# Attention sums of the even layer taken for two tiles of queries at once, and the base weight block of the MLPs loaded two pieces ahead

## The chip, the cores and the metric

One core of a Trainium2 chip runs the whole program. The metric is the device time of one execution in microseconds (us), from the first instruction to the end; the profile's span is the part from the first to the last instruction of the engines.

## The reference

A two-layer encoder trunk on 256 tokens of width 1024. The even layer runs two groups of eight heads side by side, neighbourhood attention and multi-head latent attention (MLA), behind one input projection and one output projection. The odd layer is a mixture of dilated windows. Each layer is followed by a squared-ReLU MLP.

```python
def even_mixer(xn, ...):
    hcat = xn @ w_in
    out_a = neighbourhood_attention(q, k, v, rpb)          # 8 heads of 64
    out_b = dense_attention(q, k, v, 96 ** -0.5)           # 8 heads, 96 wide keys, 64 wide values
    return jnp.concatenate([out_a, out_b], axis=-1) @ w_o

def sq_relu_mlp(xn, w1, w2):
    return jnp.square(jax.nn.relu(xn @ w1)) @ w2
```

## The kernel before

Activations stay on the core with features on the 128 partitions and 256 tokens along the free axis, which are two tiles of 128 queries. Weights come from HBM in pieces of up to 1 MB. A product of full precision is made of three products of halves: `split` (L204) makes a high part on ScalarE and the remainder on VectorE, and `mm3` (L208) multiplies high by high, high by low and low by high. These matmuls use the whole 128 by 128 array.

**The even layer** (`even`, L564) runs two lists of steps that are woven into each other by cost estimates at its end. The main list holds the projections of the heads and then `out_steps` (L328), the output projection. The side list comes from `attention` (L834) and has 16 items in `items`: eight of the neighbourhood group (kind 0) and eight of MLA (kind 1), each for one tile `t` of 128 queries and one pair `hp` of heads. An item goes through three steps. `scores` (L783) multiplies queries by keys, adds the bias of kind 0, and normalises: VectorE reduces, ScalarE takes the exponential and scales, and the result is the tile `pp`. `turn_probs` (L812) transposes `pp` with four matmuls against the identity `ident`, and one copy brings the result to the tile `pts`. `mix` (L820) multiplies the values by `pts`: the two heads of the pair use one half of the array's columns each (64 of 128), and `split` then writes 128 columns to `mixed`, which `out_steps` reads. Scores of kind 0 (`two_heads`, L213) use the array as two halves of 64 rows; scores of kind 1 use all 128 columns and 96 rows through `mm3`.

```python
for n in range(len(items) + 2):
    for fn, m in ((scores, n), (turn_probs, n - 1), (mix, n - 2)):
```

**The MLPs** (`mlp`, L355) take their second weight in seven products for eight blocks, and so need sums of blocks. For pieces `j < 14` `load_weight` (L136) fetches the fourth block of 512 columns, the base, into a tile `sums` (three buffers, tag `sum`), GpSimd copies it beside itself, and a second transfer on GpSimd's queue adds two other blocks while it writes (`accum_op=ALU.add`). `weight` (L196) hands out a piece and asks `prefetch` to load `LOAD_AHEAD` = 4 pieces ahead and to split two ahead.

The order on each engine is not that of the program text: a scheduler places each instruction where its inputs and buffers are there by its own estimates, and an earlier place in the text counts only between instructions that could both go. `open_accs`, `bank("w")` and the like draw from rings of buffers.

Of the kernel before, what the change touches and what calls it, by code (L numbers as in the profile page):

```python
# [19 lines left out]
F32 = mybir.dt.float32  # L20
# [6 lines left out]
P = 128  # L27
D = 1024
KT = D // P
T = 256  # L30
NT = T // P
# [10 lines left out]
BLK = 512  # L42
LOAD_AHEAD = 4
# [6 lines left out]
def trunk(ctx, tc, a, out):  # L50
    nc = tc.nc
# [8 lines left out]
    def scratch(shape, name):  # L60

        n = int(np.prod(shape))
        v = work.tile([P, 512], F32, tag="scratch", name=name, bufs=12)[:, :n]
        if len(shape) == 2:
            v = v.rearrange("p (a b) -> p a b", b=shape[1])
        return v
# [8 lines left out]
    def quarter_pair(name):  # L75
        return [act.tile([P, KT // 2, T], F32R, tag="quarter", name=name + v, bufs=4) for v in "hl"]

    def bank(tag):
        return ps.tile([P, 512], F32, tag=tag, name=tag)
# [26 lines left out]
    specs = []  # L106
# [25 lines left out]

    parts = {}
    state = {"loaded": 0, "split": (0, 0), "used": 0, "pool": None, "parts_done": None}

    def load_weight(pieces=1, before=lambda i: None):  # L136
        j = state["loaded"]
        src, n, _, seven = specs[j]
        if seven:

            blocks = src.rearrange("p (b n) -> p b n", n=BLK)
            sums = state["pool"].tile([P, 2, BLK], F32, tag="sum", name="sum", bufs=3)
            nc.sync.dma_start(sums[:, 0, :], blocks[:, 3, :])
            nc.gpsimd.tensor_copy(out=sums[:, 1, :], in_=sums[:, 0, :])  # L144
            nc.gpsimd.dma_start(sums, blocks[:, 0:3:2, :], accum_op=ALU.add)
            n = 3 * BLK
        raw = wraw.tile([P, WCH], F32, tag="raw", name="raw")
        for i in range(pieces):
            c = slice(i * n // pieces, (i + 1) * n // pieces)
            before(i)  # L150
            nc.sync.dma_start(raw[:, c], src[:, c])
        parts[j] = [raw, None, None] + ([sums] if seven else [])
        state["loaded"] = j + 1
# [5 lines left out]
    def split_piece(eng=None):  # L159
        j, i = state["split"]  # L160
        _, _, n, seven = specs[j]
        state["split"] = (j, i + 1) if i < n - (not seven) else (j + 1, 0)
        if i == 0:
            parts[j][1:3] = (wsp.tile([P, WCH], F32R, tag=v, name=v) for v in ("whi", "wlo"))
            if seven:

                with tc.issue_after(state["parts_done"]):
                    more_sums(parts[j])
        if i == n:
            parts[j][1:3] = split_sums(parts[j])  # L170
            return
        raw, hi, lo = (z[:, cut(j, i, n)] for z in parts[j][:3])
        return split(hi, lo, raw, eng)
# [16 lines left out]
    def prefetch(loads, splits):  # L190
        while state["loaded"] < min(loads, len(specs)):
            load_weight()
        while state["split"] < (min(splits, len(specs)), 0):
            split_piece()

    def weight():  # L196

        j = state["used"]
        prefetch(j + 1, j + 1)
        prefetch(j + LOAD_AHEAD, j + SPLIT_AHEAD)  # L200
        state["used"] = j + 1
        return parts.pop(j)[1:3]

    def split(hi, lo, src, eng=None):  # L204
        a = nc.scalar.copy(hi, src).ins  # L205
        return a, (eng or nc.vector).tensor_tensor(lo, src, hi.bitcast(F32), op=ALU.subtract).ins  # L206
# [22 lines left out]
    def tok(t):  # L229
        return slice(t * P, (t + 1) * P)  # L230
# [333 lines left out]
    def even(ep):  # L564
# [208 lines left out]
        mixed = [quarter_pair("oa"), None]  # L773
        items = [(0, t, hp) for hp in range(4) for t in range(NT)] + [(1, t, hp) for hp in range(4) for t in range(NT)]
        biases, probs, turned = {}, {}, {}
# [7 lines left out]
        def scores(n):  # L783
            kind, t, hp = items[n]
            load_bias(n + 2)

            sb = [bank("w")[:, 0:T] for _ in range(2)] if kind == 0 else bank("w").rearrange("p (j n) -> p j n", j=2)
            s_of = lambda j: sb[j] if kind == 0 else sb[:, j]
            if kind == 0:
                two_heads(sb, *qk[hp], tok(t))  # L790
            else:
                for j in range(2):
                    h = 2 * hp + j
                    (qh, ql), (kh, kl) = mT["q"], mT["k"]
                    mm3(sb[:, j], qh[0:96, h, tok(t)], ql[0:96, h, tok(t)], kh[0:96, h, :], kl[0:96, h, :], True, True)
            pp, sn = scratch([2, T], "pp"), scratch([2, T], "sn")
            mn, z, rz = (work.tile([P, 2], F32, tag=v, name=v, bufs=3) for v in ("mn", "z", "rz"))
            for j in range(2):
                o = s_of(j)
                if kind == 0:  # L800
                    nc.vector.tensor_tensor_reduce(out=sn[:, j], in0=o, in1=biases[n][:, j, :], op0=ALU.add, op1=ALU.min,
                                                   scale=-1.0, scalar=3e38, accum_out=mn[:, j:j + 1])
                else:
                    nc.vector.tensor_scalar(sn[:, j], o, -MLA_SCALE, None, ALU.mult, ALU.min, accum_out=mn[:, j:j + 1])
            for j in range(2):
                nc.scalar.activation(pp[:, j], sn[:, j], AF.Exp, bias=mn[:, j:j + 1], scale=-1.0, accum_out=z[:, j:j + 1])
            nc.vector.reciprocal(rz, z)
            for j in range(2):
                nc.scalar.activation(pp[:, j], pp[:, j], AF.Copy, scale=rz[:, j:j + 1])
            probs[n] = pp  # L810
# [7 lines left out]
            nc.any.tensor_copy(out=turned[n], in_=pt.rearrange("p (b n) -> p b n", b=4))  # L818

        def mix(n):  # L820
            kind, t, hp = items[n]
            pts = turned.pop(n)
            if mixed[kind] is None:
                mixed[kind] = quarter_pair("ob")
            v = (vna, vml)[kind]
            pvo = bank("acc" if n < 6 else "w")
            for kk in range(NT):
                for j in range(2):
                    h = 2 * hp + j
                    nc.tensor.matmul(pvo[64 * j:64 * j + 64, 0:P], v[:, kk, h * 64:(h + 1) * 64], pts[:, 2 * j + kk, :],  # L830
                                     start=kk == 0, stop=kk == NT - 1)
            split(*(z[:, hp, tok(t)] for z in mixed[kind]), pvo[:, 0:P])

        def attention():  # L834

            out = []
            for n in range(len(items) + 2):
                for fn, m in ((scores, n), (turn_probs, n - 1), (mix, n - 2)):
                    if 0 <= m < len(items):
                        out.append(lambda fn=fn, m=m: fn(m))  # L840
                if n == 0:
                    out += [lambda: None] * 2
            return out
# [322 lines left out]
```

## Time and profile before

| | |
|---|---|
| median of 3 runs | 733.68 us (733.67 to 734.14) |
| the profiled execution: its time, its span | 733.63 us, 731.9 us |
| granted TensorE clock over the span | 0.998 |
| busy over the span: TensorE, weight loads | 723.1 us, 660.6 us |
| VectorE, ScalarE, GpSimd | 623.0 us, 522.6 us, 78.8 us |
| bytes read from HBM | 142.10 MB |

The even layer takes the first 112 us, its MLP and the hand-over the time to about 300 us, the odd layer goes to about 560 us and the second MLP to the end. The matmul rows give a start and a modelled length: the length of a lone row is longer than the distance to the next start, since matmuls overlap, so times are read from start to start. A row with "x8" is eight matmuls of one line in a row; a product of 32-bit operands with `pts` shows twice, so that the four matmuls of one `mix` are a row of eight.

### The profile page before, as it was taken

The page shows a single profiled execution, that of the slowest core. Times are in us where ns is not written, and L with a number is a line of the kernel's source. Part 1 is how long each engine was busy: PE and PEld are TensorE (multiplying, and loading weights), DVE is VectorE, ACT ScalarE, POOL GpSimd, SP SyncE. Part 2 cuts the span into 40 slices and gives each one's busy share as a digit, 9 for nine tenths or more (in the row PEclk, how much of TensorE's full clock was granted, in tenths as well). Part 3 has the DMA queues.
Part 4 walks back from the last instruction along what each step waited for, and adds up shares of the span by engine and source line. Part 5 has one row for each costly group of instructions (what it writes and reads, how often), then busy time and mean ns, then how long its engine had stood idle before and what let it go on. Part 6 is the DMA issues. An engine that isn't in the chain of part 4 may idle for free.

```text
span 731.9 us, 13834 instructions
## 1 busy us (share of the span) xinstructions
PE 723.1 (99%) x5234; PEld 660.6 (90%) x5234; DVE 623.0 (85%) x1188; ACT 522.6 (71%) x986; POOL 78.8 (11%) x73
## 2 busy tenths in 40 slices
PE   9999999999999999999999999999999999999996
PEld 6988899999999998989899899998999999999995
DVE  6888859999999959989777888778759998999956
ACT  7778968767767756878676767867658766766752
POOL 0100002224222000000000000000002422232000
PEclk9999999999999999999999999999999999999999
DMA  8773338798989644664655456455658798898611
GB/s 317 274 264 133 116 116 216 216 287 244 265 263 255 193 165 166 216 207 150 229 178 171 170 188 211 170 188 198 199 195 201 235 277 221 259 273 242 211 39 59
DMA packets 38499, 149.56 MB, mean 204 GB/s; under 512 B 5152, under 2 KB 7200, under 8 KB 29344
## 3 DMA queue, kind: packets, MB, share of 16 engines
q1 hardware_dynamic: 30384, 133.71, 52.0%
q0 software_dynamic: 7616, 14.68, 12.0%
q8 instruction: 41, 0.67, 0.4%
q10 hardware_dynamic: 432, 0.28, 0.1%
q14 instruction: 26, 0.21, 0.1%
HBM read 142.10 MB, written 1.05 MB: 196 GB/s over the span
## 4 chain that ended last, share of the span: by engine, by line
PE 83%; issue 10%; DVE 3%; DMA 2%; ACT 1%; POOL 0%; SPq 0%; POOLq 0%; DVEq 0%; ACTq 0%
PE acc L937 11%; PE acc L209 10%; PE w L209 10%; PE w L210 10%; PE w L211 10%; PE acc L210 10%; PE acc L211 9%; PE acc L938 5%; PE w L218 1%; PE w L1014 1%; DMA sum<-in_w 1%; PE acc L1029 1%; PE w L816 1%; PE w L830 1%; DMA raw<-in_w_cv 1%
## 5 line engine op out<-in xcount | busy, mean ns | idle before, releaser
L206 DVE TENSOR_TENSOR wlo<-raw,whi 128x512 fp32r<-128x512 f32 (+3 forms) x360 | 296.7, 845 | 51.3 <-ACT whi L205 51.1
L205 ACT CAST whi<-raw 128x512 fp32r<-128x512 f32 (+3 forms) x360 | 253.6, 746 | 86.7 <-PE w L210 59.0
L210 PE MATMUL w<-xx,whi 128*128 128x256 f32 x528 | 149.6, 283 | 0.0
L211 PE MATMUL w<-xx,wlo 128*128 128x256 f32 x528 | 149.3, 283 | 0.0
L209 PE MATMUL w<-xx,whi 128*128 128x256 f32 x528 | 148.9, 283 | 0.0
L937 PE MATMUL acc<-xx,whi 128*128 128x512 f32 x336 | 122.0, 404 | 0.0
L210 PEld LDWEIGHTS w<-xx,whi 128*128 128x128 f32 x528 | 101.2, 192 | 1.5 <-DVE xx L246 0.4
L209 PEld LDWEIGHTS w<-xx,whi 128*128 128x128 f32 x528 | 101.0, 192 | 1.1
L211 PEld LDWEIGHTS w<-xx,wlo 128*128 128x128 f32 x528 | 101.2, 192 | 0.0
L938 PE MATMUL acc<-xx,wlo 128*128 128x256 f32 x336 | 94.3, 281 | 0.0
L144 POOL COPY sum<-sum 128x512 f32<-128x512 f32 x28 | 42.2, 1523 | 461.6 <-DVE wlo L206 279.2
L937 PEld LDWEIGHTS acc<-xx,whi 128*128 128x128 f32 x336 | 63.1, 188 | 14.1
L938 PEld LDWEIGHTS acc<-xx,wlo 128*128 128x128 f32 x336 | 63.5, 189 | 0.0
L209 PE MATMUL acc<-whi,xx 128*128 128x384 f32 (+2 forms) x160 | 55.6, 350 | 0.0
L210 PE MATMUL acc<-wlo,xx 128*128 128x384 f32 (+2 forms) x160 | 55.2, 345 | 0.1
L211 PE MATMUL acc<-whi,xx 128*128 128x384 f32 (+2 forms) x160 | 54.7, 342 | 0.0
L205 ACT CAST hh<-h 128x896 fp32r<-128x896 f32 (+1 forms) x32 | 28.9, 904 | 24.2 <-DVE h L382 23.2
L209 PE MATMUL w<-whi,hh 128*128 128x512 f32 (+1 forms) x108 | 42.1, 390 | 0.0
L210 PE MATMUL w<-wlo,hh 128*128 128x512 f32 (+1 forms) x108 | 41.5, 384 | 0.0
L211 PE MATMUL w<-whi,hl 128*128 128x512 f32 (+1 forms) x108 | 41.2, 382 | 0.0
L206 DVE TENSOR_TENSOR hl<-h,hh 128x896 fp32r<-128x896 f32 (+1 forms) x32 | 35.6, 1112 | 0.0
L206 DVE TENSOR_TENSOR suml<-sum,sumh 128x1024 fp32r<-128x1024 f32 x28 | 34.0, 1214 | 0.0
(234 smaller groups left out, 1544.4 us busy)
## 6 DMA issues: line engine op xcount, KB each, us to landing
raw<-in_w SPq DMA_DIRECT2D x36, 1024.0 KB, 5.1
raw<-in_w_oqk SPq DMA_DIRECT2D x24, 1024.0 KB, 4.9
raw<-in_w SPq DMA_DIRECT2D x28, 768.0 KB, 4.9
sum<-in_w POOLq DMA_DIRECT2D x28, 512.0 KB, 7.8
raw<-in_w_ov SPq DMA_DIRECT2D x16, 768.0 KB, 4.4
sum<-in_w SPq DMA_DIRECT2D x28, 256.0 KB, 5.7
sw<-qk SPq DMA_DIRECT2D x84, 64.0 KB, 2.6
raw<-in_w_oe SPq DMA_DIRECT2D x4, 1024.0 KB, 6.1
```

The lines of the kernel that those rows point to most:

```text
L144: nc.gpsimd.tensor_copy(out=sums[:, 1, :], in_=sums[:, 0, :])
L205: a = nc.scalar.copy(hi, src).ins
L206: return a, (eng or nc.vector).tensor_tensor(lo, src, hi.bitcast(F32), op=ALU.subtract).ins
L209: nc.tensor.matmul(o, sh, mh, start=first, stop=False)
L210: nc.tensor.matmul(o, sh, ml, start=False, stop=False)
L211: nc.tensor.matmul(o, sl, mh, start=False, stop=last)
L218: nc.tensor.matmul(o[j], y[pb, 0, ts], z[pb, 1, :], start=n == 0, stop=n == 2)
L816: nc.tensor.transpose(pt[:, b * P:(b + 1) * P], pp[:, b // 2, (b % 2) * P:(b % 2 + 1) * P], ident)
L830: nc.tensor.matmul(pvo[64 * j:64 * j + 64, 0:P], v[:, kk, h * 64:(h + 1) * 64], pts[:, 2 * j + kk, :], start=kk == 0, stop=kk == NT - 1)
L937: nc.tensor.matmul(two(pq), wh[:, ws], xT[:, k], start=k == 0, stop=False)
L938: nc.tensor.matmul(pq[:, T:2 * T], wl[:, ws], xh[:, k, :], start=False, stop=k == KT - 1)
L1014: nc.tensor.transpose(pt[:, b * P:(b + 1) * P], pp[:, at:at + P], ident)
```

## The change

`mix` is now called once for both tiles of a pair of heads: eight products into one bank and one `split` of 256 columns where there were two of four products with a `split` of 128 columns each. `attention` puts this `mix` into one step with the `scores` of a later item. `scores` writes the exponential over its input (`pp` and `sn` are one tile). `load_base` takes the load of the base and GpSimd's copy out of `load_weight`, and `weight` calls it for the piece `LOAD_AHEAD + 1` ahead while it hands out an MLP piece.

```diff
+    bases = {}
+    def load_base(j):
+        sums = state["pool"].tile([P, 2, BLK], F32, tag="sum", name="sum", bufs=3)
+        nc.sync.dma_start(sums[:, 0, :], specs[j][0][:, 3 * BLK:4 * BLK])
+        nc.gpsimd.tensor_copy(out=sums[:, 1, :], in_=sums[:, 0, :])
+        bases[j] = sums
...
-            sums = state["pool"].tile([P, 2, BLK], F32, tag="sum", name="sum", bufs=3)
-            nc.sync.dma_start(sums[:, 0, :], blocks[:, 3, :])
-            nc.gpsimd.tensor_copy(out=sums[:, 1, :], in_=sums[:, 0, :])
+            if j not in bases:
+                load_base(j)
+            sums = bases.pop(j)
             nc.gpsimd.dma_start(sums, blocks[:, 0:3:2, :], accum_op=ALU.add)
...
+        ahead = j + LOAD_AHEAD + 1
+        if ahead < len(specs) and specs[ahead][3] and specs[j][0].tensor.name in ("in_w1", "in_w2"):
+            load_base(ahead)
...
-            pp, sn = scratch([2, T], "pp"), scratch([2, T], "sn")
+            pp = sn = scratch([2, T], "pp")
...
-            for kk in range(NT):
-                for j in range(2):
-                    h = 2 * hp + j
-                    nc.tensor.matmul(pvo[64 * j:64 * j + 64, 0:P], v[:, kk, h * 64:(h + 1) * 64], pts[:, 2 * j + kk, :],
-                                     start=kk == 0, stop=kk == NT - 1)
-            split(*(z[:, hp, tok(t)] for z in mixed[kind]), pvo[:, 0:P])
+            for t in range(NT):
+                pts = turned.pop(n - 1 + t)
+                for kk in range(NT):
+                    for j in range(2):
+                        h = 2 * hp + j
+                        nc.tensor.matmul(pvo[64 * j:64 * j + 64, tok(t)], v[:, kk, h * 64:(h + 1) * 64], pts[:, 2 * j + kk, :],
+                                         start=kk == 0, stop=kk == NT - 1)
+            split(*(z[:, hp, :] for z in mixed[kind]), pvo[:, 0:T])
...
-                for fn, m in ((scores, n), (turn_probs, n - 1), (mix, n - 2)):
-                    if 0 <= m < len(items):
-                        out.append(lambda fn=fn, m=m: fn(m))
+                now = [(scores, n)] + [(mix, n - 2)] * (n % 2 and n > 2)
+                for step in (now, [(turn_probs, n - 1)]):
+                    step = [(fn, m) for fn, m in step if 0 <= m < len(items)]
+                    if step:
+                        out.append(lambda step=step: [fn(m) for fn, m in step])
```

How this moves instructions is seen at three places. **First, TensorE in the neighbourhood group.** `acc<-pts,vna` are the products of `mix`, `w<-qk_h` and its two fellows those of `scores`, and `acc<-xx,whi` a projection. Before, one `mix` of one tile and the scores behind it:

```order
L210 MATMUL acc<-xx,whi 128x256
L211 MATMUL acc<-xx,wlo 128x256
L830 MATMUL acc<-pts,vna 64x128 x4
L218 MATMUL w<-qk_h 128x256 x2
L218 MATMUL w<-qk_l,qk_h 128x256 x2
L218 MATMUL w<-qk_h,qk_l 128x256 x2
L209 MATMUL acc<-xx,whi 128x256
```

With the change, the first `mix`, of two tiles:

```order
L221 MATMUL acc<-xx,whi 128x256
L222 MATMUL acc<-xx,wlo 128x256
L229 MATMUL w<-qk_h 128x256 x2
L229 MATMUL w<-qk_l,qk_h 128x256 x2
L229 MATMUL w<-qk_h,qk_l 128x256 x2
L843 MATMUL acc<-pts,vna 64x128 x8
L220 MATMUL acc<-xx,whi 128x256
```

Eight products stand together where four stood, and they follow the scores where they preceded them. Over the whole even layer the 64 products of `mix` stood in 17 separate groups (15 of four, and one that was cut in two) and stand in 12: five pairs of tiles have become one group of eight, and the other three pairs still lie in two, two and three groups. The eight groups of 64-row scores remain; three of them touch a `mix` before and after.

**Second, ScalarE near the end of the even layer.** `CAST whi<-raw 128x1024` is the high part of the first MLP piece, `CAST obh<-w` that of a `mix`, `COPY pts<-w` brings transposed probabilities to a `mix`. Before:

```order
L806 ACTIVATE pp,z<-sn,mn 128x256 x2
L205 CAST whi<-raw 128x1024
L809 ACTIVATE pp<-pp,rz 128x256 x2
L205 CAST whi<-raw 128x1024
L205 CAST obh<-w 128x128
L806 ACTIVATE pp,z<-sn,mn 128x256 x2
L205 CAST obh<-w 128x128
L809 ACTIVATE pp<-pp,rz 128x256 x2
L818 COPY pts<-w 128x512
```

With the change:

```order
L817 ACTIVATE pp,z<-pp,mn 128x256 x2
L216 CAST obh<-w 128x256
L820 ACTIVATE pp<-pp,rz 128x256 x2
L216 CAST whi<-raw 128x1024 x2
L817 ACTIVATE pp,z<-pp,mn 128x256 x2
L829 COPY pts<-w 128x512
L820 ACTIVATE pp<-pp,rz 128x256 x2
L817 ACTIVATE pp,z<-pp,mn 128x256 x2
L216 CAST obh<-w 128x256
```

Two casts of 1024 columns stand together ahead of two exponentials and of the copy that the second tile of a `mix` needs.

**Third, SP's queue in the first MLP.** `sum<-in_w` is the load of a base, `raw<-in_w` that of a weight piece. Before:

```order
L151 DMA raw<-in_w 128x1536
L143 DMA sum<-in_w 128x512
L151 DMA raw<-in_w 128x2048
L143 DMA sum<-in_w 128x512
L151 DMA raw<-in_w 128x1536
L151 DMA raw<-in_w 128x2048
L143 DMA sum<-in_w 128x512
```

With the change:

```order
L159 DMA raw<-in_w 128x1536
L140 DMA sum<-in_w 128x512
L159 DMA raw<-in_w 128x2048
L159 DMA raw<-in_w 128x1536
L140 DMA sum<-in_w 128x512
L159 DMA raw<-in_w 128x2048
L140 DMA sum<-in_w 128x512
```

The sixth base goes one weight piece later. The 27 other bases of the two MLPs keep their places between the weight pieces, and on GpSimd the 28 copies and the 28 adding transfers stand in the order in which they stood. The part of the change that has to do with bases, taken alone, leaves the order on all five engines as it was; the swap of the sixth base comes with the other part.

## Rows read from the trace of the kernel before

**Rows 1.** Page: busy time, chain that ended last.

```profile
PE 723.1 (99%) x5234; PEld 660.6 (90%) x5234; DVE 623.0 (85%) x1188; ACT 522.6 (71%) x986; POOL 78.8 (11%) x73
...
PE 83%; issue 10%; DVE 3%; DMA 2%; ACT 1%; POOL 0%; SPq 0%; POOLq 0%; DVEq 0%; ACTq 0%
```

**Rows 2.** Waits of TensorE over the span, longest first: us in total, times, longest.

```profile
PE acc L90 <- DVE warm L85: 1.2, 1, 1.2
PE w L287 <- DVE diag L280: 0.2, 1, 0.2
```

**Rows 3.** Busy time by stage: even layer, first MLP.

```profile
27.00:112.00 85.00, 85.00 (x721) 76.43 (x721) 67.07 (x205) 68.36 (x183) 4.09 (x7) 1.00 0.45 158
112.00:300.00 188.00, 187.74 (x1236) 173.24 (x1234) 173.59 (x243) 133.90 (x190) 33.71 (x27) 1.00 0.77 227
```

**Rows 4.** Timeline of PE, a mix alone: start, length, operation.

```profile
95.33 0.28 PE L210 MATMUL acc<-oal,whi 128*128 128x256 f32 x1
95.45 0.28 PE L211 MATMUL acc<-oah,wlo 128*128 128x256 f32 x1
95.66 0.66 PE L830 MATMUL w<-pts,vml 128*64 128x128 f32 x8
96.25 0.39 PE L209 MATMUL w<-kh,qh 96*128 96x256 f32 x1
96.47 0.28 PE L210 MATMUL w<-kl,qh 96*128 96x256 f32 x1
```

**Rows 5.** The same group, windows that cut off its first pairs.

```profile
95.82 0.50 PE L830 MATMUL w<-pts,vml 128*64 128x128 f32 x6
95.93 0.38 PE L830 MATMUL w<-pts,vml 128*64 128x128 f32 x3
```

**Rows 6.** Timeline of PE, a mix that touches 64-row scores.

```profile
52.58 0.28 PE L211 MATMUL acc<-xx,wlo 128*128 128x256 f32 x1
52.78 0.66 PE L830 MATMUL acc<-pts,vna 128*64 128x128 f32 x8
...
54.14 0.28 PE L210 MATMUL acc<-xx,whi 128*128 128x256 f32 x1
```

**Rows 7.** Timeline of PE, products just before and behind 64-row scores (six) alone.

```profile
38.95 0.28 PE L211 MATMUL acc<-xx,wlo 128*128 128x256 f32 x1
...
39.93 0.28 PE L210 MATMUL acc<-xx,whi 128*128 128x256 f32 x1
```

**Rows 8.** Casts and copies, by shape: count, busy us, mean ns, idle before.

```profile
L205 ACT CAST obh<-w 128x128 fp32r<-128x128 f32 x8 | 2.1, 261 | 0.9 <-PE w L830 0.8
L205 ACT CAST oah<-acc 128x256 fp32r<-128x256 f32 x4 | 1.5, 374 | 1.0 <-PE acc L1034 0.9
L818 ACT COPY pts<-w 128x512 f32<-128x512 f32 x5 | 2.9, 584 | 1.0 <-PE w L816 1.0
```

**Rows 9.** Timeline of PE, hand-over to the first MLP.

```profile
118.51 0.28 PE L209 MATMUL w<-xx,whi 128*128 128x256 f32 x1
118.82 0.39 PE L210 MATMUL w<-xx,whi 128*128 128x256 f32 x1
```

**Rows 10.** Timelines of SP, POOL, ACT, PE: the sixth base, a later weight piece.

```profile
145.92 0.33 SPq L143 DMA_DIRECT2D sum<-in_w  x1
149.54 0.33 SPq L151 DMA_DIRECT2D raw<-in_w  x1
...
170.23 1.05 ACT L205 CAST sumh<-sum 128x1024 fp32r<-128x1024 f32 x1
...
188.66 0.39 PE L209 MATMUL acc<-sumh,hh 128*128 128x512 f32 x1
```

**Rows 11.** DMA issues: size, median us from issue to landing.

```profile
raw<-in_w SPq DMA_DIRECT2D x36, 1024.0 KB, 5.1
```

**Rows 12.** Timeline of ACT, where the casts of the first MLP piece begin.

```profile
97.73 0.51 ACT L806 ACTIVATE pp<-sn,mn 128x256 f32<-128x256 f32 x1 [0.97 <-DVE sn L804]
...
98.73 1.03 ACT L205 CAST whi<-raw 128x1024 fp32r<-128x1024 f32 x1
```

More of the change, by code (lines that the diff above doesn't have):

```diff
@@ L820, in mix @@
         def mix(n):
-            kind, t, hp = items[n]
-            pts = turned.pop(n)
+            kind, _, hp = items[n]
             if mixed[kind] is None:
```

## Prediction, made before the changed kernel ran

> **What bounds the kernel now.** I read the page first: busy time, then the chain that ended last. TensorE is busy 99% of the span, and the chain lies on it for 83%; the 10% called issue are again TensorE's own time between records [rows 1]. Next come the waits of TensorE, longest first: one of 1.2 us at the start, the next 0.2 us [rows 2]. After the start TensorE waits for nothing worth a term. Then busy time by stage: in the even layer VectorE is busy 67 of 85 us and ScalarE 68, in the first MLP 174 and 134 of 188 [rows 3]. Both have air, and the granted clock is 1.00 there, the 2.4 GHz level. So the time is the sum of TensorE's steps from start to start, and an edit counts only if it changes those steps or makes TensorE wait. Last I read TensorE's timeline around single groups of `mix`, where the change works [rows 4 to 7].
>
> **The profiled run against the median.** The profiled execution took 733.63 us, the median is 733.68. I work on the former and add 0.05. What a measurement can tell from no change is 0.2%, here 1.47 us, so faster begins below 732.21.
>
> **Term 1: changes of the array's shape.** Take a `mix` between products that use the whole array. The product ahead starts at 95.45, the second one behind it at 96.47 [rows 4]: 1.02 us. Two ordinary steps of 0.12 (95.33 to 95.45) leave 0.78 for the group. It has four pairs of matmuls. One window cuts off the first pair and one the next, and their first starts are 95.82 and 95.93 [rows 5]: 0.11 a pair, 0.44 for four. The other 0.34 are not work: 0.17 on the way in and 0.17 on the way out. Where the `mix` touches the scores of 64 rows, both together take 54.14 − 52.58 − 0.24 = 1.32 [rows 6]. Such scores alone take 39.93 − 38.95 − 0.24 = 0.74 [rows 7]. Apart the two would be 0.78 + 0.74 = 1.52, so touching saves 0.20: one change less. A change thus costs 0.17 to 0.20 us.
>
> The count comes from the order. Before, 17 groups of `mix` and 8 of 64-row scores, of which three touch: 2 × 25 − 3 = 47 changes. With the change, 12 and 8, three touching: 2 × 20 − 3 = 37. Ten fewer are 1.7 us by rows 4 and 5, and 2.0 by rows 6 and 7. The touching groups are few, so I take a value near the lower end: **1.8 us off**. The products themselves are the same 64, at the same 0.11 a pair.
>
> Two things the trace does not show. First, the three touches are `mix` then scores before, and scores then `mix` now. From below, this direction saves nothing and 3 × 0.20 = 0.6 is lost again; from above it saves as much as the other. I take the latter, because the nearest row is the opposite crossing between the same two shapes. The Trainium skill, page TensorEngine Tiling (Array Packing), says in its key properties that changing the tiling mode, and not just the tile, drains TensorE; by that the direction is of no account and the sum is the ten changes of above. No run here shows the direction yet. Second, the second tile's four products begin again in the other half of the bank. From above such a restart costs nothing; from below it costs 0.05, half a pair's step, in each of five joined groups, 0.25 in all. I take nothing, since a group of eight records already runs evenly [rows 5].
>
> **Term 2: the eviction.** Sixteen casts of 128 columns at 261 ns become eight of 256 columns, whose nearest row is a cast of that shape at 374 ns [rows 8]: 4.2 us of ScalarE become 3.0, with a like saving on VectorE. TensorE's steps cover this, so it is worth **0**. If that cover is gone, one cast is 0.11 us longer. For the last `mix`, the output projection needs the result after 11 products (11 × 0.12 = 1.3 us), where seven stood before; the longer cast fits there.
>
> **Term 3: the scores in place.** `pp` and `sn` as one tile removes a buffer and no instruction: **0**. The exponential already follows its reduction [rows 12].
>
> **Term 4: the bases.** The part alone moves nothing on any engine. `sum` still has three buffers, and the scheduler already issued the loads as early as these allow. That the change doesn't do what it says is, for this half, not a rival but my forecast: **0**. What moves, by the other half's doing, is the sixth base: its issue at 145.92 now falls behind a weight piece at 149.54 [rows 10], 3.6 us later. Its cast stood at 170.23 and its first product at 188.66 [rows 10], so 3.6 us are hidden in 24. On SP the swapped pieces pass each other; a 1 MB piece takes 5.1 us to land [rows 11], and the one that now goes first only gains. On GpSimd, copies and adding transfers keep their order, so nothing queues anew. If the copy were late, the adding transfer, the cast on ScalarE and then the product would be, in that order.
>
> **Term 5: the hand-over.** One product starts at 118.51 and the next at 118.82 [rows 9]: 0.31 in place of 0.12, so 0.19 are idle. With the even layer shifted this may vanish or grow by about 0.3. I take 0 and keep ±0.3 for the range.
>
> **Sum:** 733.63 − 1.8 + 0 + 0 + 0 + 0 = 731.8, with the 0.05 **731.9 us**.
>
> **Rival A, ScalarE's queue.** Where two casts of 1024 columns stand ahead of two exponentials and of the copy for a second tile, the queue holds 2 × 1.03 + 2 × 0.51 + 0.58 = 3.7 us [rows 8, 12]. From the last product of the scores to the second tile's products, TensorE has 12 products (1.44), four transposes (0.44, at a pair's step), six products (0.72), a change (0.17) and the first tile (0.44): 3.2 us. If the casts start only as the scores end, TensorE waits 0.5; a weight piece late by another 1.3 gives back the whole gain. Time: 732.4 to 733.7. Against it: the exponential waited 0.97 us for VectorE before [rows 12], which is slack for the casts. Chance 0.10.
>
> **Rival B, the new sequence saves less.** Scores then `mix` saves nothing (0.6 back) and the second tile restarts (0.25 back): 1.8 − 0.85 = 0.95 off, 732.7. For it: neither is in the trace. Chance 0.08.
>
> **Rival C, one bank for both tiles.** All eight products now fill one bank, which one cast and one remainder empty. If the next scores need that bank's successor before it is emptied, TensorE stands for a cast of 0.37 and about as much on VectorE, an estimate from the same row [rows 8]: 0.7 us once, 732.6. Against it: TensorE has no such wait now, with two evictions for one [rows 2]. The Trainium skill, page Perfetto Trace Analysis, section Optimizing Tensor Performance, wants independent groups of matmuls to rotate through banks so that the emptying of one overlaps the next; by that rule both tiles in one bank is the worse way. Chance 0.03.
>
> **Rival D, slower.** The casts of the first MLP piece stand on ScalarE ahead of the last items' exponentials and copies. Should the piece land late, ScalarE blocks there, the transposed probabilities come late, and TensorE stands in the last `mix`. The price is at most the landing of one piece, 5.1 us [rows 11]: 733.7 − 1.8 + 5.1 = 737.0. It decides from a wait of 3.3 us on TensorE (1.8 eaten and 1.5 more). Against it: before, the first of these casts ran at 98.73 straight behind an exponential, with no wait for a transfer [rows 12], and loads are issued as early as buffers allow. Chance 0.05.
>
> **How the numbers follow.** The forecast keeps 0.74, A 0.10, B 0.08, C 0.03, D 0.05. The low end: 2.0 off and 0.3 off the hand-over, with 0.05 added, is 731.4; less half a microsecond, as one of the three runs differs by 0.46, 730.9. The high end takes in B, C and nearly all of A: 733.4. Left out are D, the worst of A and a larger gain. Faster by over 0.2% holds the forecast alone: 0.74. B, C and A lie above 732.21 and are no difference that can be told: 0.21. D is slower: 0.05.
>
> **What the profile after would show.** If right: TensorE's waits are again one of 1.2 us at the start and none with a sum behind it; a joined group of eight products runs to about 0.78 + 0.44 = 1.22 us from start to start, less ordinary steps; scores with a `mix` of two tiles behind take 1.32 + 0.44 = 1.76; the even layer ends about 1.8 us earlier, and everything behind is as long as before. Wrong if: scores then `mix` shows 0.20 more (B); TensorE waits on `pts` and ScalarE is the releaser (A, or D if a transfer is behind that); TensorE waits on a `w` bank behind a remainder (C); the MLPs change length, which would make the bases worth something. A gain much above 2.3 us would mean that a join is worth more than two changes of shape.

## The result and the profile after

The changed kernel takes **735.9 us** (median of 9 runs, 734.97 to 737.25) against 733.7 for the kernel before (9 runs, 733.51 to 734.25): a ratio of 1.0029, 95% interval 1.0019 to 1.0039. The forecast was 731.9 with a range from 730.9 to 733.4. The profiled execution is the fastest of the nine, 734.97 us with a span of 733.2.

Busy time and the chain that ended last, on the page of the changed kernel, beside [rows 1]:

```profile
PE 722.7 (99%) x5234; PEld 662.4 (90%) x5234; DVE 619.8 (85%) x1179; ACT 521.0 (71%) x979; POOL 86.7 (12%) x73
...
PE 69%; issue 12%; DVE 12%; POOL 2%; DMA 2%; ACT 1%; POOLq 0%; DVEq 0%; SPq 0%; ACTq 0%
```

TensorE has as much work as before, but the chain leaves it: VectorE holds 12% where it held 3%, GpSimd 2% where it held none. GpSimd is busy 7.9 us longer with the same 28 copies and transfers. TensorE's waits, longest first, beside [rows 2]:

```profile
PE w L220 <- ACT relu L384: 2.0, 1, 2.0
PE acc L90 <- DVE warm L85: 1.2, 1, 1.2
```

One new wait of 2.0 us. Where does it lie? TensorE's timeline of the kernel before has the first product of the first MLP's second weight and the first transposition behind that MLP:

```profile
133.11 0.48 PE L209 MATMUL w<-whi,hh 128*128 128x512 f32 x1
...
278.90 0.52 PE L436 MATMUL w<-ident,y 128*128 128x128 f32 x3
```

The same two in the changed kernel, and between them the wait and the products behind it:

```profile
130.97 0.48 PE L220 MATMUL w<-whi,hh 128*128 128x512 f32 x1
...
177.79 0.39 PE L222 MATMUL acc<-sumh,hl 128*128 128x512 f32 x1
180.19 0.38 PE L220 MATMUL w<-xx,whi 128*128 128x256 f32 x1 [2.01 <-ACT relu L384]
...
182.10 0.41 PE L221 MATMUL w<-xx,whi 128*128 128x256 f32 x1
182.32 0.41 PE L222 MATMUL w<-xx,wlo 128*128 128x256 f32 x1
...
280.55 0.52 PE L447 MATMUL w<-ident,y 128*128 128x128 f32 x3
```

The even layer and the hand-over became 2.14 us shorter (133.11 to 130.97). Between the two marks the first MLP became 3.79 us longer (145.79 to 149.58). The step at 177.79 is 2.40 us, some 2.2 more than an ordinary one. Behind it products start 0.22 apart, not 0.12. Busy time by stretch says why (the column PEclk, the third from the end, is the granted clock):

```profile
180.00:183.00 3.00, 2.81 (x15) 2.81 (x16) 2.96 (x5) 3.00 (x5) 0.00 (x0) 0.61 0.78 292
183.00:186.00 3.00, 3.00 (x23) 3.00 (x23) 3.00 (x6) 1.95 (x3) 0.22 (x1) 0.82 0.23 52
186.00:190.00 4.00, 4.00 (x26) 3.58 (x25) 4.00 (x6) 2.10 (x3) 1.62 (x2) 1.00 0.71 214
```

After the wait the clock fell to its 1.2 GHz level (from 180.8 us on, by the steps) and came back some 3 us later, at 184.0. The wait (2.2) and this stretch (1.6) make up the 3.8 us. What lies behind the second mark is 0.35 us shorter than before, so the two profiles differ by 1.3 us. The medians differ by 2.2; the other 0.9 us lie in executions without a profile, and no trace shows where.

Now back from the wait. GpSimd's timeline in the kernel before, with its copy of the sixth base at 151.29:

```profile
151.29 0.80 POOL L144 COPY sum<-sum 128x512 f32<-128x512 f32 x1 [3.58 <-DMA sum<-in_w]
152.39 1.09 POOL L145 DMA_DIRECT2D sum<-in_w  x1 [0.30 <-POOL sum L144]
...
172.70 4.35 POOL L144 COPY sum<-sum 128x512 f32<-128x512 f32 x1 [8.45 <-DVE wlo L206]
```

The same place in the changed kernel:

```profile
154.19 9.94 POOL L141 COPY sum<-sum 128x512 f32<-128x512 f32 x1 [8.14 <-DMA sum<-in_w]
164.43 1.09 POOL L153 DMA_DIRECT2D sum<-in_w  x1 [0.30 <-POOL sum L141]
```

A copy that takes 0.8 us took 9.94, and the adding transfer behind it on GpSimd's queue went out at 164.43. VectorE's timeline over the same time:

```profile
153.75 0.68 DVE L188 TENSOR_TENSOR every<-raw 128x512 f32<-128x512 f32 x1
154.35 1.21 DVE L217 TENSOR_TENSOR wlo<-raw,whi 128x1024 fp32r<-128x1024 f32 x1
...
162.97 0.68 DVE L188 TENSOR_TENSOR every<-raw 128x512 f32<-128x512 f32 x1
170.87 0.69 DVE L187 TENSOR_TENSOR raw<-sum,raw 128x512 f32<-128x512 f32 x1 [7.21 <-issue]
```

VectorE runs without a gap from before 153.75 to 163.65, each instruction starting before the one ahead has quite ended. The copy ends 0.5 us after VectorE stops, at 164.13. Then VectorE itself stands 7.2 us, since its next instruction reads `sum`, which the late adding transfer fills (it lands 6.4 us after its issue at 164.43). In the kernel before the same instruction has no wait:

```profile
166.07 0.68 DVE L179 TENSOR_TENSOR raw<-sum,raw 128x512 f32<-128x512 f32 x1
```

There the adding transfer, issued at 152.39, landed 6.2 us later, 7.5 us before VectorE came to this instruction. That is all that the sixth sum has in hand. In the changed kernel what is queued behind it on VectorE (`h`, `hl`) is late, then ScalarE, which stands 4.4 us for `h` and so comes late to `relu`, then TensorE:

```profile
176.40 0.95 ACT L216 CAST hh<-h 128x896 fp32r<-128x896 f32 x1 [4.41 <-DVE h L393]
```

### The profile page after: what moved, and what is told of

The parts are those of the page before. It is cut to its first block, busy times and chain, and to the rows that moved or that the text cites. A ratio compares the mean times of both kernels' runs of the same rounds, so it can differ in the third digit from the quotient of the medians.

```text
span 733.2 us, 13811 instructions
## 1 busy us (share of the span) xinstructions
PE 722.7 (99%) x5234; PEld 662.4 (90%) x5234; DVE 619.8 (85%) x1179; ACT 521.0 (71%) x979; POOL 86.7 (12%) x73
## 4 chain that ended last, share of the span: by engine, by line
PE 69%; issue 12%; DVE 12%; POOL 2%; DMA 2%; ACT 1%; POOLq 0%; DVEq 0%; SPq 0%; ACTq 0%
PE acc L953 11%; PE acc L220 9%; PE acc L221 9%; PE acc L222 9%; PE w L221 6%; PE w L220 6%; PE w L222 6%; PE acc L954 5%; DVE wlo L217 5%; DVE suml L217 2%; DMA sum<-in_w 2%; POOL sum L141 2%; PE w L229 1%; PE w L1030 1%; PE acc L1045 1%
## 5 line engine op out<-in xcount | busy, mean ns | idle before, releaser
L141 POOL COPY sum<-sum 128x512 f32<-128x512 f32 x28 | 50.7, 1810 | 459.0 <-DMA sum<-in_w 413.3
```

## The experiments

Two theories. **Copy theory**: VectorE keeps GpSimd's copy off for as long as it runs two-input instructions from SBUF back to back, and that copy carried the loss. **Late-load theory**: the sixth base is simply loaded too late.

### The two halves of the change

The attention half alone is the changed kernel less this:

```diff
-        ahead = j + LOAD_AHEAD + 1
-        if ahead < len(specs) and specs[ahead][3] and specs[j][0].tensor.name in ("in_w1", "in_w2"):
-            load_base(ahead)
```

> Only the attention half of the change; the bases are loaded as before. Its order on every engine is that of the whole change, the sixth base's load behind a weight piece included. Both theories (the copy on GpSimd is kept off by VectorE; the sixth base's load is simply late) and the statement that the base half does nothing want the time of the whole change, 735 to 737 us, with a GpSimd copy of several us between 150 and 165 us. If the base half is at fault: about 731.6.

Measured: 735.37 us (734.08 to 737.88), ratio 1.0024 (1.0013 to 1.0036), and in the profile:

```profile
154.38 10.08 POOL L141 COPY sum<-sum 128x512 f32<-128x512 f32 x1 [8.00 <-DMA sum<-in_w]
```

TensorE's wait is there too, and a little longer, but the granted clock behind it stays at 1.00:

```profile
180.79 0.39 PE L217 MATMUL w<-xx,whi 128*128 128x256 f32 x1 [2.28 <-ACT relu L381]
```

```profile
180.00:183.00 3.00, 2.21 (x18) 2.21 (x19) 2.96 (x5) 3.00 (x5) 0.00 (x0) 1.00 0.89 363
```

This execution is the shortest of its ten. So the stretch at the lower clock does not follow every wait of this length. Over the ten the granted clock goes from 0.998 to 0.994, and the longest (737.88) is the one with the lowest.

The bases alone are `load_base` and the three lines in `weight` on the kernel before:

```diff
+            if j not in bases:
+                load_base(j)
+            sums = bases.pop(j)
...
+            load_base(ahead)
```

> Only the base half of the change on the kernel before; the order on every engine is as before. If the base half does nothing: 733.7 (733.4 to 734.3). If it costs what the whole change lost in the first MLP (3.8 us): about 737.5.

Measured: 733.9 us, ratio 1.0001 (0.9992 to 1.0011). The base half does nothing by itself. The long copy and the loss come with the attention half.

### The sixth base without GpSimd's copy

```diff
-        nc.gpsimd.tensor_copy(out=sums[:, 1, :], in_=sums[:, 0, :])
+        if sum(seven for *_, seven in specs[:j]) == 5:
+            nc.sync.dma_start(sums[:, 1, :], specs[j][0][:, 3 * BLK:4 * BLK])
+        else:
+            nc.gpsimd.tensor_copy(out=sums[:, 1, :], in_=sums[:, 0, :])
```

> The whole change, but the sixth base's second copy comes by a second load of the same block and not by GpSimd; all else stays in its order, and the first load of the sixth base is as late as in the changed kernel. Copy theory (VectorE keeps the copy off for 9.94 us): the wait of 2.0 us on TensorE and the stretch at the lower clock behind it go, the first MLP takes as long as before, 733.7 - 2.1 = 731.6 us (731.2 to 732.2). Late-load theory: the load lands at the same 154 us and the sums stay late, 735 to 737 us.

In the next run the second line is `nc.scalar.copy(sums[:, 1, :], sums[:, 0, :])`.

> The whole change, but the sixth base is copied by ScalarE and not by GpSimd, one copy of 128x512 that stands behind a cast of the sums; no further transfer. Copy theory: the copy takes about 0.6 us whatever VectorE does, and the time is near 731.6 us (731.2 to 732.4). Late-load theory, or if any copy at that time were stretched: 735 to 737 us.

Measured: 731.47 us, ratio 0.9965 (0.9952 to 0.9978), and 731.74 us, 0.9972 (0.9962 to 0.9982). The copy on ScalarE, and the adding transfer behind it:

```profile
155.03 0.62 ACT L142 COPY sum<-sum 128x512 f32<-128x512 f32 x1 [4.95 <-DMA sum<-in_w]
155.96 1.09 POOL L156 DMA_DIRECT2D sum<-in_w  x1 [8.88 <-ACT sum L142]
```

The load lands as late as in the changed kernel (155.0), but the copy takes 0.62 us and the adding transfer goes out 8.5 us earlier. TensorE's new wait is gone in both. The late-load theory falls. With the copy out of the way the change is worth 2.0 to 2.3 us, near the 2.14 that the even layer and the hand-over gave in the trace.

### The copy measured by itself

A small program: VectorE works through chains while GpSimd copies 128x512 once beside each. Its core:

```diff
+    def both_sbuf():
+        for i in range(10):
+            nc.vector.tensor_tensor(outs[i], a1, a2, op=ALU.subtract)
+    def one_psum():
+        for i in range(18):
+            nc.vector.tensor_tensor(outs[i][:, 0:512], bank, a2[:, 0:512], op=ALU.subtract)
```

> Not the trunk: a small program that measures the disputed cost by itself, and its output holds two of VectorE's results. A GpSimd copy of 128x512 starts while VectorE works through a chain without a pause, one phase each: nothing beside it; subtractions of two SBUF tiles, 1024 columns (12 us in all) and 512 columns; subtractions with one input in PSUM; one-input multiplications from SBUF; the first chain with one wait for ScalarE in its middle; the first chain with each instruction waiting for VectorE's own earlier ones. Copy theory: 0.6 us alone; beside two SBUF inputs the copy ends only behind the chain (8 us or more), or in the pause for ScalarE (some 5 us); beside one input in PSUM 0.6 to 1.4 us. If the copy's length came from DMA traffic or from the weights' landing and not from VectorE: 0.6 to 1.2 us in all phases, as there is no traffic here.

GpSimd's copies in the order of the phases: alone (the first of two), two SBUF inputs with 1024 and with 512 columns, one input in PSUM, one input from SBUF, a pause for ScalarE, a wait for its own results:

```profile
8.34 0.61 POOL L105 COPY dst<-src 128x512 f32<-128x512 f32 x1 [7.89 <-ACT src L102]
...
10.62 1.27 POOL L105 COPY dst<-src 128x512 f32<-128x512 f32 x1 [0.53 <-ACT src L102]
22.46 10.97 POOL L105 COPY dst<-src 128x512 f32<-128x512 f32 x1 [10.56 <-ACT src L102]
33.96 0.61 POOL L105 COPY dst<-src 128x512 f32<-128x512 f32 x1 [0.53 <-ACT src L102]
44.79 0.74 POOL L105 COPY dst<-src 128x512 f32<-128x512 f32 x1 [10.21 <-ACT src L102]
56.10 5.81 POOL L105 COPY dst<-src 128x512 f32<-128x512 f32 x1 [10.58 <-ACT src L102]
67.94 11.49 POOL L105 COPY dst<-src 128x512 f32<-128x512 f32 x1 [6.02 <-ACT src L102]
```

With no DMA traffic the copy takes 0.61 us alone and beside an input in PSUM, 0.74 beside one input from SBUF, and 5.8 to 11.5 us beside two. It ends in the pause, or behind the chain. This is the copy theory, but for the first chain, where the copy got in after one subtraction (1.27 us). A second small program took that up, with six chains of 14 subtractions of 512 columns:

```diff
+        for i in range(14):
+            nc.vector.tensor_tensor(outs[first + (i if k < 3 else i % 3)], a1, a2, op=ALU.subtract)
```

> Not the trunk: the small program again, six chains of 14 subtractions of two SBUF tiles of 512 columns, a copy on GpSimd beside each that starts at three different points of the chain; the first three chains hold no semaphore wait, the last three have one that is long met in each instruction from the fourth on. If a chain without waits lets a copy in at the first boundary, as the first chain of the earlier small program did (1.27 us), and one with met waits does not (11 us there): 0.7 to 1.3 us three times, then some 7 us three times. If the point of arrival decides: long and short copies among both kinds.

```profile
7.35 0.73 POOL L75 COPY dst<-src 128x512 f32<-128x512 f32 x1 [6.91 <-ACT src L72]
16.51 8.31 POOL L75 COPY dst<-src 128x512 f32<-128x512 f32 x1 [8.43 <-ACT src L72]
25.78 0.92 POOL L75 COPY dst<-src 128x512 f32<-128x512 f32 x1 [0.96 <-ACT src L72]
34.26 8.57 POOL L75 COPY dst<-src 128x512 f32<-128x512 f32 x1 [7.57 <-ACT src L72]
43.62 1.08 POOL L75 COPY dst<-src 128x512 f32<-128x512 f32 x1 [0.79 <-DVE o L74]
52.70 8.14 POOL L75 COPY dst<-src 128x512 f32<-128x512 f32 x1 [7.99 <-ACT src L72]
```

Long and short alternate, so neither the semaphore waits nor the point of arrival decides alone. In both small programs the four short copies beside two SBUF inputs meet a chain ahead of which VectorE had just stood (0.03 to 1.0 us), and the six long ones a chain that followed VectorE's work before it without a gap. The next run does not fit that, so which chain lets a copy in stays open. What holds in these runs: a copy that does not get in at once stays out until VectorE stops.

### The swap alone, on the kernel before

```diff
+            with tc.issue_after(state["fifth"]) if k == 5 else ExitStack():
+                nc.sync.dma_start(sums[:, 0, :], blocks[:, 3, :])
...
```

(`state["fifth"]` is the weight transfer that stood behind the sixth base.)

> The kernel before with one edit: the sixth base's load is issued behind the weight piece that followed it; every other place in every engine's order is kept. My step said that 3.6 us more are hidden in 24: 733.7 us. Copy theory: the load lands near 155 us, in a stretch where VectorE runs from 153 to 162 us without a pause, and the copy takes 4 to 8 us where it took 0.8; whether TensorE then waits depends on the sums' slack: 733.7 to 737 us.

Measured: 733.8 us, ratio 1.0001 (0.9991 to 1.0011). The copy began at 156.38 and took 0.79 us, where 4 to 8 were expected: it got in at once, though VectorE had run without a gap since before 148 us. So the swap as such cost nothing here, and a chain without a pause is not enough for a long copy; the loss needs a copy that does not get in. The runs of this kernel spread from 733.08 to 735.36, much as those of the kernel before measured beside it (733.43 to 735.27).

### All bases loaded twice

The same replacement of the copy for all 28 bases, without the condition.

> The whole change, but no base is copied by GpSimd: all 28 are loaded twice (7.3 MB more from HBM). Copy theory: the long copies in both MLPs go; TensorE waited for none but the sixth, so the time is that of the run with the sixth alone loaded twice, 731.5 us (731.0 to 732.2), and runs of the same kernel differ less. If the added traffic delays weights, or if the copies paced something else: over 732.5 us.

Measured: 732.32 us, ratio 0.9976 (0.9967 to 0.9985), a little above the expected band and below the other theory's. The runs do not differ less than before (731.38 to 732.94). In the profile, of the slowest run, 1.5 us are lost in the first ten microseconds, ahead of any base, where products of 512 columns start 0.43 us apart and not 0.23; from there it runs with the kernel that loads the sixth twice, to within 0.4. So no gain shows from removing the other long copies.

### More pairs joined

To the kernel with the sixth base loaded twice, the eight products of a `mix` tied together:

```diff
+            def product(t, kk, j):
...
+            one = product(1, 0, 0)
+            with tc.issue_after(getattr(one, "ins", one)):
+                for t, kk, j in ((1, 0, 1), (1, 1, 0), (1, 1, 1), (0, 0, 0), (0, 0, 1), (0, 1, 0), (0, 1, 1)):
+                    product(t, kk, j)
```

> The whole change with the sixth base loaded twice, and the eight products of every mix tied together, the late tile's first: the 12 groups become 9 (one pair is still cut). My term of 0.17 to 0.20 us for a change of shape: three groups less are six changes less, 1.0 to 1.2 us, 730.4 us (730.0 to 731.0). If the even layer's gain came from something else (the number of groups being of no account): 731.5 us. Slower if TensorE now waits for the late tile's copies.

Measured: 732.12 us, ratio 0.9979 (0.997 to 0.9989), not faster than the 731.47 without the tie. The profile shows one wait that could be the cause:

```profile
66.73 0.54 PE L845 MATMUL acc<-pts,vna 128*64 128x128 f32 x5 [0.78 <-DVE pts L832]
```

The third `mix` now waits for its late tile. Without the tie on that one:

> The whole change with the sixth base loaded twice, and the products of every mix tied together but for the third one, whose late tile made TensorE wait 0.8 us. Ten groups where the changed kernel has 12: two joins. One join took 0.35 us off in the trace of the changed kernel (two groups of eight records with 0.78 us each, one of 16 with 1.21). 731.5 - 0.7 = 730.8 us (730.4 to 731.3). If the scheduler's new places around the tied groups cost as much as they save, as with all pairs tied: 731.5 to 732.2 us.

Measured: 731.02 us, ratio 0.996 (0.9946 to 0.9974). That is 0.45 below the kernel without joins, where 0.7 was expected, and the intervals overlap: the direction fits, the size is not settled.

### A pause on VectorE, and a surprise

GpSimd's copies kept, with a stop of VectorE for the sixth base:

```diff
+        if sum(seven for *_, seven in specs[:j]) == 5:
+            flag, seen = (work.tile([P, 1], F32, tag=v, name=v, bufs=1) for v in ("flag", "seen"))
+            nc.gpsimd.tensor_copy(out=flag, in_=sums[:, 1, 0:1])
+            nc.vector.tensor_scalar(seen, flag, 1.0, None, ALU.mult)
```

> The whole change, GpSimd's copies kept, with one pause for the sixth base alone: a GpSimd copy of one column behind the base's copy, and a VectorE instruction of one column that waits for it, behind the third subtraction of h (157.8 us in the changed kernel); every other place in the order is kept. Copy theory: the copy gets in when VectorE stops there, some 4 us after the load has landed and not 9.9, the adding transfer goes out near 159 us, and what VectorE later waits for it shrinks from 7 us to about 2, which TensorE does not see: 731.6 us (731.2 to 732.6). If a pause of VectorE were of no account to the copy, VectorE would stand until a copy of its usual length under load ends, near 164 us, and the time would be 735 to 739 us.

Measured: **726.73 us**, ratio 0.99 (0.9886 to 0.9915), 5 us below what any theory said. TensorE's steps of 256 columns were shorter all over the program (0.116 us for 0.120 in the stretch from 200 to 270 us). The two small tiles had moved the weights and all that lies behind them in SBUF by 64 bytes. So the pause was tried without the shift:

```diff
+    pad = work.tile([P, 48], F32, tag="pad", name="pad", bufs=1)
+    nc.gpsimd.memset(pad, 0.0)
```

> The kernel with the pause on VectorE, and 192 unused bytes a partition ahead of the scratch tiles, so that the weights lie 256 bytes behind their place in the changed kernel and not 64: the same place within 256 bytes. Copy theory: the pause alone gives the time of the run with the sixth base loaded twice, 731.5 us (731.0 to 732.5). If the pause itself was worth the 726.7 us: again 726 to 727.5. If it does nothing for the copy and all came from the shift: 735 to 737.

Measured: 730.82 us, ratio 0.9956 (0.994 to 0.9973), 0.2 below the copy theory's range and far from the other two. GpSimd and VectorE at the pause:

```profile
155.00 4.13 POOL L143 COPY sum<-sum 128x512 f32<-128x512 f32 x1 [10.08 <-DMA sum<-in_w]
159.19 0.19 POOL L146 COPY flag<-sum 128x1 f32<-128x1 f32 x1
159.68 1.09 POOL L159 DMA_DIRECT2D sum<-in_w  x1 [0.30 <-POOL flag L146]
```

```profile
158.37 0.28 DVE L399 TENSOR_TENSOR h<-h 128x128 f32<-128x128 f32 x1
159.41 0.15 DVE L147 TENSOR_SCALAR seen<-flag 128x1 f32<-128x1 f32 x1 [0.76 <-POOL flag L146]
...
166.19 0.69 DVE L193 TENSOR_TENSOR raw<-sum,raw 128x512 f32<-128x512 f32 x1 [0.37 <-DMA sum<-in_w]
```

The copy ended 0.5 us after VectorE stopped at 158.65, as in the changed kernel, only five microseconds sooner; VectorE gave up 0.76 us and later waited 0.37 where it had waited 7.2. One stop undoes the loss with the copy left on GpSimd. And the shift without the pause, a `pad` of 16 columns, on the changed kernel, on the kernel before, and on the seven joined pairs:

> The changed kernel with 64 unused bytes a partition ahead of the weights and nothing else: all orders are kept, GpSimd's copy is not helped. If the place of the weights shortens TensorE's steps (0.117 in place of 0.120 for 256 columns, as the run with the pause showed), the time falls by about 4.8 us from the changed kernel's 735.9, to 731.1 us (730 to 733), and the long copy and TensorE's wait in the first MLP are still there. If the place is of no account: 735 to 737 us.

> The kernel before with the same 64 unused bytes and nothing else. If the place shortens the steps in any version: 733.8 - 4.8 = 729.0 us (728 to 730). If it works only together with the pause: 733.8 us.

> Seven pairs joined and the sixth base loaded twice, with the same 64 unused bytes: the parts added up are 731.0 - 4.8 = 726.2 us (725.3 to 727.2). If the gains don't add, since VectorE becomes the bound: 727.5 or more, with waits of TensorE on remainders of weights.

Measured: 729.57 us (ratio 0.994, 0.9925 to 0.9955), 727.45 (0.9914, 0.9899 to 0.9929) and **725.08 us** (0.9875, 0.986 to 0.989). All three lie 0.2 to 0.6 us below their ranges: the shift is worth more than the 4.8 us expected. The first still has its copy of 9.82 us and a wait of 2.6 us on TensorE: with the shift, too, the changed kernel is the slower one, by 2.1 us. The last is the fastest version of this study. TensorE's 48 products of one weight piece, from the first to the product behind, in the seven joined pairs without the shift:

```profile
209.51 0.28 PE L223 MATMUL w<-xx,whi 128*128 128x256 f32 x1
...
215.26 0.40 PE L223 MATMUL w<-whi,hh 128*128 128x512 f32 x1
```

and with it:

```profile
207.59 0.28 PE L225 MATMUL w<-xx,whi 128*128 128x256 f32 x1
...
213.05 0.39 PE L225 MATMUL w<-whi,hh 128*128 128x512 f32 x1
```

48 steps took 5.75 us and take 5.46: 0.120 and 0.114 us each. Three runs asked whose place it is. All are the seven joined pairs with `pad` ahead of the token tiles `xx` and `hh` (16, 16 and 48 columns), the first with another 48 columns ahead of the weights:

> Seven pairs joined and the sixth base loaded twice (731.0 us), with the token tiles (xx, hh, oah, which stream past the weights in most products) 64 bytes further and the weights 256 bytes further, which is their old place within 256 bytes. If the place of the weights alone shortened the steps: 731.0 us (730.5 to 732). If the place of the streamed tiles, or how the two lie to each other, matters: 725 to 727 us.

> The same kernel with token tiles and weights both 64 bytes further. If the weights' place alone matters: 725.1 us as in the run with the weights shifted (723.8 to 726). If what counts is how the two lie to each other: back at 731.0 us. If both operands gain by themselves: under 723 us.

> The same kernel with both 192 bytes further, so that they start at multiples of 256 bytes where the shift by 64 put them at 128. If a multiple of 128 is what counts: as with both shifted by 64, within 0.5 us. If 256: faster by another 2 us or more.

Measured: 730.35 us (0.9953, 0.9939 to 0.9968), 731.05 (0.9964, 0.9952 to 0.9977) and 730.74 (0.9959, 0.9944 to 0.9973). With both moved, the gain is gone, and with the tokens moved against the weights the other way (by 64 bytes, the weights by 256) it does not come. So it is not the place of the weights, nor a multiple of 128 or 256 bytes, but how weights and tokens lie to each other. (`pad` also moves other tiles that lie behind it; the products whose step changed read only tokens and weights.)

## Why the prediction was wrong

**The mechanism of term 1 was right.** The changed kernel's first joined group of the neighbourhood, with the products ahead and behind:

```profile
50.62 0.28 PE L222 MATMUL acc<-xx,wlo 128*128 128x256 f32 x1
...
51.38 1.09 PE L843 MATMUL acc<-pts,vna 128*64 128x128 f32 x16
52.40 0.39 PE L220 MATMUL acc<-xx,whi 128*128 128x256 f32 x1
52.62 0.28 PE L221 MATMUL acc<-xx,whi 128*128 128x256 f32 x1
```

52.62 − 50.62 − 0.24 = 1.76 us, as forecast to the hundredth. So scores ahead of a `mix` save the change of shape as the other direction does [rows 6], and rival B falls. The Trainium skill, page TensorEngine Tiling (Array Packing), key properties, makes no difference of direction, and the trace agrees with the 1.76. A lone joined group takes 1.21 in the trace, where 1.22 was forecast. Term 1 gave 2.06 us, where 1.8 stood: the first `w<-xx,whi` behind the even layer starts at 115.15 before and at 113.09 in the changed kernel. That is the upper end of the ten changes, 2.0. **Term 5**, put at nothing, gave 0.08: the step of 0.31 us [rows 9] is gone, but one of 0.19 stands at 113.45.

**Terms 2 and 3 held.** No wait on a bank or a cast appears, and A, C and D did not happen: the even layer came out shorter than forecast.

**Term 4 failed**, at the sentence that 3.6 us "are hidden in 24". It took the sixth base's load to be the only thing that moves, and carried over the copy's duration with it. It also counted the 24 us to the wrong reader. 188.66 is TensorE's first product with the sum, but the first to read the sum is VectorE's `raw<-sum` at 166.07, with 7.5 us in hand, and all that VectorE does later stands behind it. The runs show in its place: the base was issued at 148.28 and not at 145.92 [rows 10], it landed 2.9 us later on the clock (151.29 and 154.19), 5 us later in the course of the MLP, and there a copy of 0.80 us became one of 9.94. So the adding transfer went out 12.0 us later on the clock, 14 in the course of the MLP; that is some 7 more than VectorE had in hand, and it stood 7.2 us. The later load alone would have fitted: with the copy on ScalarE the transfer went out at 155.96, and VectorE did not wait for it. The forecast even listed the order in which things would be late if the copy were, but gave the copy no price, and TensorE was reached another way: not by the product of the sum, but by `h` and `relu`. A row that warned of it stood in the trace of before: a copy of 4.35 us at 172.70, seven times its length alone, with no wait behind it. It would not have given the 9.94 either. Of the signs listed, "the MLPs change length" came, but not because the bases are worth something: their half alone measured 733.9. The order also held a hint that was passed over: the release of the buffer for the sixth base is VectorE's `suml<-sum` of the third, and in VectorE's own order that instruction had moved back.

The Trainium skill, page SBUF — State Buffer, section "SBUF: two separate sides", says that VectorE and GpSimd share one pair of ports, that a VectorE instruction with two SBUF inputs holds it against a GpSimd instruction that reads SBUF, and that the loser is blocked while the other's instruction lasts. The small program agrees on which instructions block (two SBUF inputs yes, an input in PSUM no: 0.61 us). The page speaks of one instruction; here the copy stayed out over 18 subtractions of 0.68 us, 10.97 us in all.

**The rivals** had one slower case, D, with ScalarE behind a late weight. The time came near it by another way, through the engine with the least work: none of the cases looked at GpSimd.

## What to carry to other kernels

A duration read from a row belongs to its neighbours, too: when a step moves, look at what the shared engine does at the new time, price the row at least by the longest of its kind in the trace, not by the one at the old place, and count the slack to whoever reads its result first. A small GpSimd copy beside a VectorE that never pauses is not a free copy; put it on another queue (731.5 to 731.7 us here) or give VectorE one stop behind it (730.8). And before two versions are compared to a few tenths of a per cent, see that their operands lie alike in memory.

## What the runs showed that was not expected

- A GpSimd copy of 0.61 us takes 8 to 11.5 us beside a chain of two-input VectorE instructions that does not stop, or 0.7 to 1.3 when it gets in at once. In six like chains long and short alternated. Why is open.
- Where weights and streamed tokens lie to each other in SBUF sets TensorE's step. Measured in the profiles between 200 and 270 us as the mean from one start to the next of the same width, with the distance from tokens to weights counted from that of the kernel before, modulo 256 bytes: 0, 119.8 ns for 256 columns and 228 for 512; 64, 116.0 and 231; 192, 117.7 and 233.6. So 64 shortens the narrower steps and lengthens the wider ones. The first holds at three places of the pair, so the distance counts. With 64 the whole program is 5.9 to 6.6 us shorter, more than the change moved either way; with 192 it is 0.7 us shorter, no more than runs of one kernel differ. Other distances, and what in the chip causes it, were not tried.
- A wait of 2.0 us on TensorE, with a step of 2.40, was followed by 3 us at the lower clock and so cost 3.8 us in all. Waits of 2.28 us (the attention half alone) and 2.55 us (the changed kernel with the shift) at the same place were followed by none in their profiles. What decides is open.
